# RWKV state of a hybrid mLSTM/RWKV-7 layer: summed in PSUM with an identity product, scaled by ScalarE

## The chip, the core and the metric

The kernel runs on one core of a Trainium2 chip. The metric is the device time of one execution in microseconds (us). Inputs and outputs are fp32 in device memory. The engines are called here as in the profile: PE (TensorE, with PEld for its weight loads), DVE (VectorE), ACT (ScalarE), POOL (GpSimd) and SP (SyncE, which issues nearly all DMAs). Each engine works through its own list of instructions strictly in order, and waits on semaphores for the others.

## The reference, cut to what matters

One layer over 512 latent tokens with a prefix of 256 context tokens, width 2048. One combined input projection feeds two groups of heads: an mLSTM (4 heads) and a RWKV-7 (16 heads of 64, in both directions). Both outputs go through one output projection, then follow a gated ConvFFN (width 5632) and a final RMSNorm. The part that the change touches is the RWKV state, a 64 x 64 matrix for each head and direction:

```
def step(s, xs):
    r_t, w_t, k_t, v_t, kk_t, a_t = xs
    s = (s * w_t[:, :, None, :]
         - einsum("bhvk,bhk->bhv", s, kk_t)[..., None] * (kk_t * a_t)[:, :, None, :]
         + v_t[..., :, None] * k_t[..., None, :])
    return s, einsum("bhvk,bhk->bhv", s, r_t)
...
kk = kk * lax.rsqrt(jnp.sum(kk * kk, axis=-1, keepdims=True) + 1e-12)
k_dir = k_r[:, :, None, :] * (1 + (a - 1) * p["r_k_a"])
y_f, s_f = rwkv7_scan(rh, hd(decay[:, :, 0]), hd(k_dir[:, :, 0]), vh, kk, hd(a[:, :, 0]), state[2], False)
y_b, s_b = rwkv7_scan(rh, hd(decay[:, :, 1]), hd(k_dir[:, :, 1]), vh, kk, hd(a[:, :, 1]), state[3], True)
```

The latent scan starts from the final state of the context's scan. The kernel does it in chunks of 64 tokens.

## The kernel before

**Stages.** The program first computes the modulation vectors and projects the context (to some 400 us of the trace), then interleaves the input projection of the 512 latent tokens with the RWKV work (to some 1400 us), finishes the RWKV and mLSTM heads, runs the output projection in two halves of its input rows (first half from 1650 us, second until 1890 us) and then the ConvFFN.

**Bulk products.** The projections (`proj` at L362, `proj_tm` at L391) split each fp32 operand in a high and a low fp32r part and do three products for each weight block: L370 to L372 with 512 columns, L403 to L405 with 256. `wload` (L337) loads a weight block from memory, ACT casts its high part (`whi`, L299), DVE subtracts to get the low part (`wlo`, L300). Below, these products up to the first of the output projection (L1262) are called bulk products; they wait for nothing of the RWKV work, so they fill PE while that is under way.

**RWKV of a head pair.** Eight pairs of heads, `p` = 0 to 7, two heads on the two halves of the partitions. Each goes through three steps:

1. `prep` (L680): decays, the running products `E1` and `E2` of them, and from them the tiles `KR` (kk and r) and `BK` (minus kk times a, and k). `gC` holds the decay over a whole chunk for each state row. `BK` is scaled by `gC` into `bg` (L756, DVE), transposed on PE (L759, 192 in all) into PSUM, copied by ACT (L763) and written to a buffer in memory (L764). The products of `BK` and `KR` (L747, masked at L750) go to memory too.
2. `tsolve` (L777), for two pairs at once: loads the triangular blocks into the tile `t_X`, inverts them with 30 pairs of DVE operations (L798, L799), then finishes each pair of heads with small PE products (L816, L821), ACT and DVE copies (L818, L823).
3. `chain` (L903): eight `chain_step`s (L841) for a latent pair, four for a context pair, each for one chunk in each direction. A step multiplies the state `u.M` and the values with the chunk's operator, ACT copies the result (`Rs`, L872), a second round of products gives `U` (ACT copy, L880), a third adds up the new state in PSUM, and DVE writes it back: `M = M * gC + sum` (L892). DVE copies out the outputs (L899, L901). There are 96 steps, 88 of them with a new state, four L892 each (352).

The pairs' chains run two at a time for the latent tokens: pairs 0 and 1 while pair 3 is prepared, 2 and 3 with pair 5, 4 and 5 with pair 7, and 6 and 7 after all preparations. The tile `t_X` of the last solve is then taken over by the mLSTM heads 0 and 1 (`mlstm_head`, L540), whose outputs the first half of the output projection needs.

**Another user of DVE.** `ada_late` (L219) computes modulation vectors for later stages: a DMA brings a block of two rows of weights into `am`, one buffer for this stretch, and DVE adds each row into `adacc` (L232, 16 rows of 512 columns for a vector). These stand in DVE's list between the RWKV's instructions.

**Order.** Each engine's list is made by the framework's scheduler, which simulates the program with costs of its own and lets an instruction stand where that simulation has it start. So taking an instruction from one engine to another shifts the lists of all of them.

Of the kernel before, what the change touches and what calls it, by code (L numbers as in the profile page):

```python
# [10 lines left out]
AF = mybir.ActivationFunctionType  # L11
ALU = mybir.AluOpType
# [3 lines left out]
P = 128  # L16
# [80 lines left out]
def body(tc, A, dbg=None):  # L97
    nc = tc.nc
    pe, dve, act, pool, sp = nc.tensor, nc.vector, nc.scalar, nc.gpsimd, nc.sync
# [22 lines left out]
    cst = Pool("cst")  # L122
# [5 lines left out]
    def PS(tag, shape):  # L128
        return ps.tile(list(shape), F32, tag=tag, name=nm(tag), bufs=PB[tag])
# [9 lines left out]
    def cload(name, shape):  # L139
        t = cst("c_" + name, shape)  # L140
        sp.dma_start(t, A[name])
        return t

    rk = Pool("rk")
    rp = Pool("rp")
# [8 lines left out]
    ident = cload("ident", [P, P])  # L154
    bones = cload("bones", [P, P])
    gmask = cload("gmask", [P, 2, P])
    reset = cload("reset", [P, NX + 1])
    bones2 = cload("bones2", [P, 2])
    bconst = cst("bconst", [P, 5])
    for j, v in enumerate((1.0, 1e-6, 1e-12, 64e-5, 0.0)):  # L160
        pool.memset(bconst[:, j:j + 1], v)
# [518 lines left out]
    def prep(p, s, seg, S_d, d=None):  # L680
# [17 lines left out]
        for j, (pt, t, vn) in enumerate(((pw, sg, "w0"), (pa, a, "a0"))):  # L698
            for i, d in enumerate(dirs):
                cs = slice(i * n, i * n + n)  # L700
                pe.matmul(pt[:, cs], s.up[:, j, d, :], (lw, la)[j][seg], start=True, stop=True)
            for i, d in enumerate(dirs):
                cs = slice(i * n, i * n + n)
# [5 lines left out]
        BK = rp("r_BK", [P, 8, 128], 1)  # L709
        E2 = sg  # L710
        gC = rk("r_gC", [P, 8], 16)
# [27 lines left out]
        for hf in range(2):  # L739
# [3 lines left out]
            for c4 in range(4):  # L743
                for h, pg in enumerate(pgs):
                    hs = LOHI[h]
# [6 lines left out]

        for hf in range(2):
            cs = slice(4 * hf, 4 * hf + 4)
            bg = rp("r_cum", [P, 4, 128])
            dve.tensor_tensor(bg, BK[:, cs, :], gC[:, cs, None].to_broadcast([P, 4, 128]), ALU.mult)  # L756
            pb = PS("pre", [P, 4, 128])
            for c4 in range(4):
                pe.transpose(pb[:, c4, :], bg[:, c4, :], ident)  # L759
            bt = rp("r_sg", [P, 4, 128])  # L760
            for h, hs in enumerate(LOHI):
                for js in LOHI:
                    act.copy(bt[hs, :, js], pb[js, :, hs])  # L763
            sp.dma_start(S[:, cs, 3 * kc:3 * kc + 128], bt)  # L764
# [4 lines left out]
        for d in dirs:  # L769
            u = Unit()  # L770
# [70 lines left out]
    def chain_step(us, ops, cs, V, y, first, last):  # L841

        x = us[0].seg == "x"
        kc = us[0].kc
        bank = [PS("R", [P, 8, 64]) for _ in range(2)]
        pos = (0, 1) if cs[0] < cs[1] else (1, 0)
        opened = {}

        def mm(h, half, o, w, rhs):

            hs = LOHI[h]
            out = bank[h][LOHI[half], o, :]
            at = opened.get((h, half))
            f = dict(stop=True, skip_group_check=True)
            if at is None:
                opened[(h, half)] = pe.matmul(out, w[hs], rhs[hs], start=True, **f)
                return
            with tc.issue_after(at.ins):
                pe.matmul(out, w[hs], rhs[hs], start=False, **f)  # L859

        w = [o[:, c % 2] for o, c in zip(ops, cs)]
        kinds = range(2) if x else range(1)
        for src in range(2):
            for k, u in enumerate(us):
                for j in kinds:
                    for h in range(2):
                        o = 2 * kc * src + 64 * j
                        mm(h, h if j == 0 else 1 - h, pos[k], w[k][:, o:o + 64], u.M if src == 0 else V[:, cs[k], :])
        Rs = rk("r_Rs", [P, 2, 64], 3)
        U = rk("r_U", [P, 2, 64], 3)  # L870
        for h, hs in enumerate(LOHI):
            act.copy(Rs[hs], bank[h][hs, 0:2, :])  # L872
        for k, u in enumerate(us):
            for h in range(2):
                mm(h, 1 - h, 2 + pos[k], w[k][:, kc:kc + 64], Rs[:, pos[k], :])
            for h in range(2):
                if not last:
                    mm(h, h, 2 + pos[k], w[k][:, 3 * kc + 64:3 * kc + 128], V[:, cs[k], :])
        for h, hs in enumerate(LOHI):
            act.copy(U[hs], bank[h][LOHI[1 - h], 2:4, :])  # L880
        for k, u in enumerate(us):
            for h in range(2):
                if not last:
                    mm(h, h, 2 + pos[k], w[k][:, 3 * kc:3 * kc + 64], U[:, pos[k], :])
            for h in range(2):
                if x:
                    mm(h, 1 - h, pos[k], w[k][:, kc + 64:kc + 128], U[:, pos[k], :])
        if not last:
            for k, u in enumerate(us):
                g = u.g0 + cs[k]  # L890
                for h, hs in enumerate(LOHI):
                    dve.scalar_tensor_tensor(u.M[hs], u.M[hs], u.gC[hs, g:g + 1], bank[h][hs, 2 + pos[k], :], ALU.mult, ALU.add)  # L892
        if x:
            lo, hi = min(cs), max(cs)
            for h in range(2):
                hs = LOHI[1 - h]
                out = y[hs, lo:hi + 1:hi - lo, :]
                if first:
                    dve.tensor_copy(out, bank[h][hs, 0:2, :])  # L899
                else:  # L900
                    dve.tensor_tensor(out, bank[h][hs, 0:2, :], out, ALU.add)  # L901

    def chain(pairs, mid):  # L903

        x = pairs[0][0].seg == "x"
        nch = pairs[0][0].nch
        Vs, ys = [], []
        for us in pairs:
            Vs.append(chain_v(us[0].p, us[0].seg, nch))
            ys.append(rk("r_yt", [P, 8, 64], 2) if x else None)  # L910
            for u in us:
                if not x:
                    Mst[(u.p, u.d)] = rk("r_M", [P, 64], 16)
                    pool.memset(Mst[(u.p, u.d)], 0.0)
                u.M = Mst[(u.p, u.d)]
        n = nch // 2
        for i in range(n):
            if x and i == 1:
                mid()
            ops = [[chain_load(u, i if u.d == 0 else n - 1 - i) for u in us] for us in pairs]  # L920
            for c in range(2 * i, 2 * i + 2):
                for us, o, V, y in zip(pairs, ops, Vs, ys):
                    chain_step(us, o, (c, nch - 1 - c), V, y, c < nch // 2, x and c == nch - 1)
        if x:
            for us, y in zip(pairs, ys):
                y_d = us[0].y_d = DT("yr_d", [4, P, 128], 8)
                for h in range(2):
                    sp.dma_start(y_d[:, :, 64 * h:64 * h + 64].rearrange("a (b t) v -> t (a b) v", t=64), y[LOHI[1 - h]])
            mid()
# [215 lines left out]
    def ctx_job(p):  # L1145
        do_chain()
        job = []
        for pp in range(p, p + 2):
            s = pair_shared(pp, "c")
            job.append((pp, prep(pp, s, "c", DT("Sc_d", [P, 8, 320], 8)), None))  # L1150
        do_solve()
        solve_q.append(job)

    def x_job(p):
        if p < 2:
            do_chain()
        elif p % 2 == 0:
            do_solve(2)
        else:
            do_chain(2)  # L1160
        s = pair_shared(p, "x")
        S_d = DT("Sx_d", [P, 16, 512], 8)
        us = prep(p, s, "x", S_d, 0) + prep(p, s, "x", S_d, 1)
        job = [(p, us, bonus(p, us[0], us[1], s))]
        if p == 0:
            do_solve()
        solve_q.append(job)
# [185 lines left out]
    last, end = [], iter(())  # L1353
# [147 lines left out]
```

## Time and profile before

| | us |
|---|---|
| median of three runs | 3376.26 |
| fastest and slowest of them | 3374.53, 3378.07 |
| profiled execution | 3379.97 |
| its span, first to last instruction | 3378.2 |
| mean granted TensorE clock | 0.945 of full |

| stretch of the span | what runs there | PE busy of the stretch, clock |
|---|---|---|
| 400 to 883 us | context RWKV, start of the latent projection | 450 of 483 us, 0.94 |
| 883 to 1364.6 us | latent projection with RWKV pairs 1 to 7 | 437 of 482 us, 0.92 and 0.87 |
| 1364.6 to 1650.3 us | last solve, last chain, mLSTM heads 0 and 1 | 170 of 286 us, 0.95 to 0.52 |
| 1650.3 to 3378.2 us | output projection, ConvFFN | 1685 of 1728 us, 0.96 and 0.99 |

PE is busy for 92% of the whole span. A busy share of PE overstates its work, because consecutive products overlap, and a granted clock of 0.5 means that the engine runs at 1.2 GHz where 1.0 is 2.4 GHz.

### The profile page before, as it was taken

The numbers are of one execution on the slowest core, as the hardware profiler recorded it, in microseconds if no ns is written. First come the engines' busy times: TensorE is split into PE (matmuls) and PEld (weight loads), VectorE is DVE, ScalarE is ACT, GpSimd is POOL, SyncE is SP. The second block draws the span as 40 slices with busy tenths as digits, with TensorE's granted clock in tenths as the row PEclk, the third lists the DMA queues.
The fourth block names the chain that finished last, engine by engine and source line by source line (L and its number), as shares of the span: only waits on it lengthen the run. The fifth ranks groups of instructions, "written<-read, shape, count | busy, mean of one in ns | idle before, by whom it ended". The sixth has DMA issues, their size and how long they took to land.

```text
span 3378.2 us, 54574 instructions
## 1 busy us (share of the span) xinstructions
PE 3108.0 (92%) x21030; PEld 2509.7 (74%) x21030; DVE 2165.9 (64%) x4178; ACT 1192.4 (35%) x2414; POOL 59.6 (2%) x113
## 2 busy tenths in 40 slices
PE   8998899999989898657599899999999999999998
PEld 5687777777768687545477688888888888888887
DVE  2587776688688778645644788455555555555657
ACT  4355554344444344222223432222222222322323
POOL 0000100010000000000000000000000000000000
PEclk9999998899989898767799999999999999999999
DMA  8877555557767687565844255222223222222232
GB/s 284 305 243 220 155 159 163 166 174 234 208 208 239 215 247 240 181 197 178 257 153 157 77 199 194 94 94 98 95 95 99 94 96 98 94 98 96 94 100 100
DMA packets 394387, 548.53 MB, mean 162 GB/s; under 512 B 151664, under 2 KB 272776, under 8 KB 393872
## 3 DMA queue, kind: packets, MB, share of 16 engines
q1 hardware_dynamic: 384480, 531.67, 49.3%
q10 hardware_dynamic: 9648, 13.37, 1.1%
q8 instruction: 166, 2.72, 0.3%
q14 instruction: 93, 0.76, 0.1%
HBM read 457.49 MB, written 87.47 MB: 161 GB/s over the span
## 4 chain that ended last, share of the span: by engine, by line
PE 53%; DMA 9%; DVE 6%; ACT 1%; issue 1%; SPq 1%; DVEq 0%; ACTq 0%
PE acc L371 10%; PE acc L372 10%; PE acc L370 10%; PE acc L1376 5%; PE acc L1378 5%; PE acc L1377 5%; DMA am<-in_wmod 3%; PE acc L1262 1%; PE pre L621 1%; PE acc L1263 1%; PE acc L1264 1%; DVE adacc L232 1%; DMA Sx_d<-r_sg 1%; PE R L859 1%; DMA x_d<-ev 1%
## 5 line engine op out<-in xcount | busy, mean ns | idle before, releaser
L299 ACT CAST whi<-wraw 128x512 fp32r<-128x512 f32 (+1 forms) x948 | 569.6, 604 | 1307.7 <-PE acc L371 678.6
L300 DVE TENSOR_TENSOR wlo<-wraw,whi 128x512 fp32r<-128x512 f32 (+1 forms) x948 | 628.4, 666 | 429.0 <-ACT whi L299 423.1
L370 PE MATMUL acc<-H,whi 128*128 128x512 f32 x1920 | 761.2, 396 | 6.1 <-ACT ev L520 4.0
L372 PE MATMUL acc<-H,wlo 128*128 128x512 f32 x1920 | 762.3, 397 | 1.2 <-DVE wlo L300 1.2
L371 PE MATMUL acc<-H,whi 128*128 128x512 f32 x1920 | 760.4, 396 | 0.0
L370 PEld LDWEIGHTS acc<-H,whi 128*128 128x128 f32 x1920 | 363.8, 189 | 87.5 <-ACT ev L520 4.3
L372 PEld LDWEIGHTS acc<-H,wlo 128*128 128x128 f32 x1920 | 364.2, 190 | 82.0 <-issue 4.9
L371 PEld LDWEIGHTS acc<-H,whi 128*128 128x128 f32 x1920 | 364.4, 190 | 78.8 <-issue 2.9
L1380 DVE SCALAR_TENSOR_TENSOR x<-acc,mod,x 128x512 f32<-128x512 f32 (+1 forms) x192 | 135.6, 706 | 221.7 <-PE acc L1378 221.6
L1324 DVE SCALAR_TENSOR_TENSOR f_cv<-upad,fvec,f_cv 128x512 f32<-128x512 f32 x352 | 263.8, 749 | 7.2
L1376 PE MATMUL acc<-fh,whi 128*128 128x512 f32 x640 | 253.2, 396 | 0.0
L1377 PE MATMUL acc<-fl,whi 128*128 128x512 f32 x640 | 253.1, 396 | 0.0
L1378 PE MATMUL acc<-fh,wlo 128*128 128x512 f32 x640 | 253.1, 396 | 0.0
L232 DVE SCALAR_TENSOR_TENSOR adacc<-am,csil,adacc 128x512 f32<-128x512 f32 x240 | 179.4, 748 | 83.7 <-DMA am<-in_wmod 81.6
L403 PE MATMUL acc<-whi,H 128*128 128x256 f32 x512 | 159.8, 313 | 2.2 <-ACT r_E L720 1.5
L405 PE MATMUL acc<-wlo,H 128*128 128x256 f32 x512 | 158.6, 311 | 1.6 <-DVE wlo L300 1.6
L404 PE MATMUL acc<-whi,H 128*128 128x256 f32 x512 | 156.0, 305 | 0.0
L1378 PEld LDWEIGHTS acc<-fh,wlo 128*128 128x128 f32 x640 | 120.2, 188 | 29.1
L1377 PEld LDWEIGHTS acc<-fl,whi 128*128 128x128 f32 x640 | 120.2, 188 | 29.0
L1376 PEld LDWEIGHTS acc<-fh,whi 128*128 128x128 f32 x640 | 120.2, 188 | 29.0
L1262 PE MATMUL acc<-H,whi 128*128 128x512 f32 x256 | 104.6, 414 | 32.4 <-DVE ev L1271 18.6
L750 DVE TENSOR_TENSOR r_Gp<-pre,c_gmask 64x512 f32<-64x512 f32 (+1 forms) x192 | 115.1, 599 | 18.1 <-DMA Sx_d<-r_Gp 11.6
(346 smaller groups left out, 4751.6 us busy)
## 6 DMA issues: line engine op xcount, KB each, us to landing
am<-in_wmod SPq DMA_DIRECT2D x128, 512.0 KB
wraw<-in_wup SPq DMA_DIRECT2D x88, 512.0 KB
wraw<-in_wgate SPq DMA_DIRECT2D x88, 512.0 KB
wraw<-in_wdn SPq DMA_DIRECT2D x88, 512.0 KB
wraw<-in_wcm SPq DMA_DIRECT2D x72, 512.0 KB
r_GK<-Sx_d SPq DMA_DIRECT2D x64, 512.0 KB
wraw<-in_wtm SPq DMA_DIRECT2D x56, 512.0 KB
Sx_d<-r_Gp SPq DMA_DIRECT2D x32, 512.0 KB
```

What stands on the lines that cost most here:

```text
L232: dve.scalar_tensor_tensor(acc, wm[:, k % 2], csil[:, k:k + 1], acc, ALU.mult, ALU.add)
L299: act.copy(hi, t)
L300: dve.tensor_tensor(lo, t, hi.bitcast(F32), ALU.subtract)
L370: pe.matmul(pt[:, :n], hi(k8), H.h(k), start=k == 0, stop=False)
L371: pe.matmul(pt[:, :n], hi(k8), H.l(k), start=False, stop=False)
L372: pe.matmul(pt[:, :n], lo(k8), H.h(k), start=False, stop=k == KT - 1)
L403: pe.matmul(o, H.h(k)[:, xs], hi(k4), start=first, stop=False, skip_group_check=True)
L405: pe.matmul(o, H.h(k)[:, xs], lo(k4), start=False, stop=k == KT - 1, skip_group_check=True)
L1324: dve.scalar_tensor_tensor(cv, u[:, a:a + GH, b:b + GW], fvec[:, f, tap:tap + 1], cv, ALU.mult, ALU.add)
L1376: pe.matmul(pt, hi(m)[:, k, :], th[:, cs], start=k == 0, stop=False)
L1377: pe.matmul(pt, hi(m)[:, k, :], tl[:, cs], start=False, stop=False)
L1378: pe.matmul(pt, lo(m)[:, k, :], th[:, cs], start=False, stop=k == GF - 1)
```

## The change

In `chain_step` the old state is added to the sum in PSUM by a product with an identity matrix (`eye2`), and ACT multiplies the whole sum by `gC` on the way back into `u.M`. DVE no longer takes part in the state. Since the sum is now scaled as a whole, `BK` must reach the chain unscaled, so the scaling into `bg` goes and PE transposes `BK` itself.

```
@@ body
+    eye2 = cst("eye2", [P, 64])
+    for hs in (slice(0, 64), slice(64, 128)):
+        pool.tensor_copy(eye2[hs], ident[hs, hs])
@@ prep
-            bg = rp("r_cum", [P, 4, 128])
-            dve.tensor_tensor(bg, BK[:, cs, :], gC[:, cs, None].to_broadcast([P, 4, 128]), ALU.mult)
             pb = PS("pre", [P, 4, 128])
             for c4 in range(4):
-                pe.transpose(pb[:, c4, :], bg[:, c4, :], ident)
+                pe.transpose(pb[:, c4, :], BK[:, 4 * hf + c4, :], ident)
@@ chain_step, after the products of V with the operator
+            for h in range(2):
+                if not last:
+                    mm(h, h, 2 + pos[k], eye2, u.M)
@@ chain_step, the new state
-                    dve.scalar_tensor_tensor(u.M[hs], u.M[hs], u.gC[hs, g:g + 1], bank[h][hs, 2 + pos[k], :], ALU.mult, ALU.add)
+                    act.activation(u.M[hs], bank[h][hs, 2 + pos[k], :], AF.Copy, scale=u.gC[hs, g:g + 1])
```

In the changed file the lines after these stand one to four lower: the transposition is L760, the new state L896, a solve's product L817.

The counts of instructions differ by this: PE has 352 more products (64 x 64, the identity), DVE has 48 `bg` and 352 state updates fewer, ACT has 352 state writes more and two more loads of its function table, POOL two copies more at the start. The bulk products are the same 4752. The lists differ from the end of the context's projection on. Three places show how.

PE's list around the last transposition of the last prepared pair, before (`pre`, `r_cum`: transposition; `R`: chain; `acc`: bulk products):

```order
L859 MATMUL R_13408<-r_V_12660,r_GK_13279 64x64
L759 MATMUL pre_13661<-c_ident_90,r_cum_13659 128x128 x4
L939 MATMUL pre_13676<-r_rk_2419_13674,r_kd_13518 128x2 x4
L403 MATMUL acc_17052<-whi_17175,H_2684 128x256
L404 MATMUL acc_17052<-whi_17175,H_2685 128x256
L405 MATMUL acc_17052<-wlo_17176,H_2684 128x256
L403 MATMUL acc_17051<-whi_17229,H_2686 128x256
```

And now:

```order
L860 MATMUL R_13485<-r_V_12811,r_GK_13478 64x64
L760 MATMUL pre_13853<-c_ident_90,r_BK_13804 128x128 x4
L760 MATMUL pre_13864<-c_ident_90,r_BK_13804 128x128 x4
L374 MATMUL acc_16854<-H_2690,whi_16895 128x512
L375 MATMUL acc_16854<-H_2689,wlo_16896 128x512
L373 MATMUL acc_16854<-H_2689,whi_16895 128x512
```

The last two transpositions of four now follow each other, and they stand earlier among the bulk products: 147 bulk products stood behind them before (96 of 512 columns, 51 of 256), now it is 389 (197 and 192).

PE's list in front of the first products of the last solve (`R<-t_X,t_Y`), before (L238 and L605 belong to `ada_late` and to mLSTM head 0):

```order
L370 MATMUL acc_17370<-H_2686,whi_17411 128x512
L371 MATMUL acc_17370<-H_2687,whi_17411 128x512
L372 MATMUL acc_17370<-H_2686,wlo_17412 128x512
L238 MATMUL pre_15893<-c_ones_80,adacc_13689 128x1 x4
L605 MATMUL pre_15996<-r_kr_15932,r_KR_15934 128x512
...
L605 MATMUL pre_16012<-r_kr_15932,r_KR_15934 128x512
L816 MATMUL R_13805<-t_X_13801,t_Y_13802 32x32
```

And now:

```order
L407 MATMUL acc_17311<-whi_17488,H_2690 128x256
L408 MATMUL acc_17311<-wlo_17489,H_2689 128x256
L406 MATMUL acc_17310<-whi_17488,H_2689 128x256
L817 MATMUL R_14008<-t_X_14004,t_Y_14005 32x32
L817 MATMUL R_14009<-t_X_14004,t_Y_14005 32x32
```

Before, no bulk product was left behind this place. Now 131 are (96 of 512 columns, 35 of 256), 99 of them (64 and 35) ahead of the solve's second pair of heads. Between the last transposition and this place stand 101 bulk products of 512 and 157 of 256 columns.

ACT's list at the first step of the last chain, before (`t_X<-R`: solve; `t_X<-t_X`: mLSTM head 0):

```order
L818 COPY t_X_13801<-R_13879 32x512
L818 COPY t_X_13801<-R_13880 32x512
L872 COPY r_Rs_13984<-R_13966 64x128
L872 COPY r_Rs_13984<-R_13967 64x128
L880 COPY r_U_13985<-R_13966 64x128
L880 COPY r_U_13985<-R_13967 64x128
L589 ACTIVATE t_X_15941<-t_X_15941 128x128
L594 ACTIVATE t_X_15941<-t_X_15941,tokb_132 128x256
```

And now:

```order
L873 COPY r_Rs_14187<-R_14170 64x128
L302 CAST whi_17940<-wraw_17938 128x512
L884 COPY r_U_14188<-R_14169 64x128
L884 COPY r_U_14188<-R_14170 64x128
L592 ACTIVATE t_X_16200<-t_X_16200 128x128
L597 ACTIVATE t_X_16200<-t_X_16200,tokb_135 128x256
L592 ACTIVATE t_X_16200<-t_X_16200 128x128
L302 CAST whi_17944<-wraw_17938 128x512
L896 ACTIVATE r_M_7521<-R_14169,r_gC_12607 64x64
L896 ACTIVATE r_M_7523<-R_14169,r_gC_12691 64x64
L896 ACTIVATE r_M_7521<-R_14170,r_gC_12607 64x64
L896 ACTIVATE r_M_7523<-R_14170,r_gC_12691 64x64
```

Weight casts now stand among the step's copies, and the state writes behind them. In DVE's list, the additions of `ada_late` keep their places beside the RWKV work: 98 stood ahead of the last solve before and 96 now, 126 and 122 ahead of its end, 170 and 170 ahead of the output projection's first result (L1271).

## Rows read from the trace of the kernel before

**Rows 1.** The page's engine line: busy us, share of the span, instructions.
```profile
PE 3108.0 (92%) x21030; PEld 2509.7 (74%) x21030; DVE 2165.9 (64%) x4178; ACT 1192.4 (35%) x2414; POOL 59.6 (2%) x113
```

**Rows 2.** Stretches: us; busy PE, PEld, DVE, ACT, POOL (instructions); clock; DMA share; GB/s.
```profile
883.00:1244.70 361.70, 327.69 (x3977) 266.19 (x3970) 286.44 (x637) 155.95 (x354) 6.80 (x20) 0.92 0.72 223
...
1244.70:1364.60 119.90, 109.57 (x1500) 89.01 (x1498) 87.86 (x200) 51.84 (x127) 2.15 (x5) 0.87 0.73 239
...
1402.10:1472.10 70.00, 22.67 (x334) 15.01 (x336) 40.90 (x90) 6.58 (x14) 0.00 (x0) 0.52 0.52 152
...
1472.10:1650.30 178.20, 112.86 (x1190) 83.38 (x1186) 93.48 (x247) 57.09 (x178) 1.72 (x8) 0.72 0.67 212
```

**Rows 3.** Waits of PE, 400 to 1400 us: total us, times, longest.
```profile
PE pre L759 <- DVE r_cum L756: 10.6, 4, 6.3
...
PE R L859 <- ACT r_U L880: 10.4, 9, 1.7
...
PE R L856 <- DVE r_M L892: 1.7, 5, 0.7
```

**Rows 4.** DVE groups, 400 to 1650 us: xcount, busy, mean ns, idle before.
```profile
L892 DVE SCALAR_TENSOR_TENSOR r_M<-r_M,r_gC,R 64x64 f32<-64x64 f32 x352 | 87.5, 278 | 28.5 <-PE R L859 21.9 <-ACT r_U L880 2.7
...
L756 DVE TENSOR_TENSOR r_cum<-r_BK,r_gC 128x512 f32<-128x512 f32 x41 | 28.1, 685 | 2.8 <-PE pre L759 2.3
```

**Rows 5.** ACT groups, 400 to 1650 us, the same columns.
```profile
L299 ACT CAST whi<-wraw 128x512 fp32r<-128x512 f32 x195 | 120.0, 618 | 187.6 <-PE acc L371 114.7 <-PE acc L404 51.4 <-DVE t_X L799 8.1
...
L763 ACT COPY r_sg<-pre 64x256 f32<-64x256 f32 x168 | 61.7, 367 | 70.8 <-PE pre L759 29.8 <-DMA Sx_d<-r_sg 25.7 <-PE acc L404 6.5
...
L880 ACT COPY r_U<-R 64x128 f32<-64x128 f32 x192 | 49.8, 260 | 80.7 <-PE R L859 75.1 <-DVE t_X L799 1.6 <-ACT ev L520 0.4
...
L872 ACT COPY r_Rs<-R 64x128 f32<-64x128 f32 x192 | 49.8, 259 | 98.6 <-PE R L859 88.5 <-DVE t_T L798 3.6 <-DVE ev L173 3.1
...
L520 ACT COPY ev<-acc 128x256 f32<-128x256 f32 x32 | 11.2, 373 | 9.2 <-DMA v_x<-ev 3.2 <-DMA vx_d<-ev 2.6 <-PE acc L405 1.6
...
L626 ACT ACTIVATE r_KR<-pre,m_dn 128x256 f32<-128x256 f32 x8 | 3.8, 472 | 8.3 <-DVE m_dn L625 8.3
```

**Rows 6.** A stretch of bulk products alone, columns as in Rows 2.
```profile
2000.00:2500.00 500.00, 500.00 (x2198) 410.20 (x2197) 304.35 (x458) 137.03 (x224) 0.00 (x0) 1.00 0.35 118
```

**Rows 7.** Timeline of PE: start us, us, engine, line, tiles, form, xcount.
```profile
1366.68 0.45 PE L859 MATMUL R<-r_Rs,r_GK 64*64 64x64 f32 x8
...
1367.06 0.38 PE L404 MATMUL acc<-whi,H 128*128 128x256 f32 x1
...
1371.99 0.28 PE L405 MATMUL acc<-wlo,H 128*128 128x256 f32 x1
...
1372.36 0.28 PE L405 MATMUL acc<-wlo,H 128*128 128x256 f32 x1
...
1471.61 0.97 PE L859 MATMUL R<-r_U,r_GK 64*64 64x64 f32 x16 [0.36 <-ACT r_U L880]
```

**Rows 8.** Timeline of PE: last transposition, last solve, start of the output projection.
```profile
1364.02 0.66 PE L759 MATMUL pre<-c_ident,r_cum 128*128 128x128 f32 x4
...
1424.95 1.84 PE L238 MATMUL pre<-c_ones,adacc 128*128 128x1 f32 x8 [22.87 <-DVE adacc L232]
...
1447.87 1.92 PE L816 MATMUL R<-t_X,t_Y 32*32 32x32 f32 x64 [9.65 <-DVE t_X L810]
...
1464.78 1.92 PE L816 MATMUL R<-t_X,t_Y 32*32 32x32 f32 x64 [11.22 <-DVE t_X L810]
...
1650.34 0.80 PE L1262 MATMUL acc<-H,whi 128*128 128x512 f32 x1 [18.55 <-DVE ev L1271]
```

**Rows 9.** Timeline of DVE: start and end of the last solve.
```profile
1372.41 0.09 DVE L794 MEMSET t_X<- 128x32 f32 x1 [1.20 <-DMA t_X<-Sx_d]
...
1470.62 1.40 DVE L823 COPY t_Y<-R 32x512 f32<-32x512 f32 x2
```

**Rows 10.** Tile adacc on DVE, 1364 to 1651 us: idle before it, times.
```profile
  DMA am<-in_wmod: 46.3, 25
```

## The prediction

> **What bounds the kernel now.** I read the engine line first: PE is busy for 92% of the span, so the time lies with PE and only its idle stretches can be shortened [rows 1]. The stretches come next. While pairs are prepared, PE is busy for 327.7 of 361.7 us and 109.6 of 119.9 us, at a clock of 0.92 and 0.87; DVE for 286.4 and 87.9, ACT for 156.0 and 51.8. From 1402.1 us the picture turns: 22.7 of 70.0 us, then 112.9 of 178.2 us, at a clock of 0.52 and 0.72, thus nearer to 1.2 than to 2.4 GHz [rows 2]. There the bulk products are used up, and PE waits: 22.87 us ahead of L238, 9.65 and 11.22 ahead of the last solve's products [rows 8]. From the end of the last solve on DVE, 1472.0 us [rows 9], it takes 178 us to the output projection at 1650.3 [rows 8]. So the end of the latent part is set by a string: last preparation (last transposition 1364.0), solve (first product 1447.9, 83.9 us later), end of the solve, mLSTM heads 0 and 1 with the last chain beside them, output projection. The bulk products lie beside it and are all done some 46 us before the solve reaches PE. What follows 1650 us is not touched by the change.
>
> While pairs are prepared PE hardly waits for what the change removes: 10.6 us for the scaled BK, 1.7 us for the new state, each over 1000 us [rows 3]. So the removed DVE work gains little directly; what counts is where it lets the lists put the RWKV work.
>
> **Part by part.**
>
> *DVE loses* 352 state updates of 278 ns, 97.9 us, and 48 scalings of 685 ns, 32.9 us [rows 4]: 131 us on an engine that is busy for three quarters of the stretch [rows 2]. Off PE's path by themselves, but the preparation and the solve run through DVE.
>
> *PE gains* 352 identity products of 64 x 64. Rows of the same form: eight take 0.38 us up to the next product, 48 ns each; sixteen took 0.97 us at the low clock, 61 ns [rows 7]. The lower end is nothing, where they fall into a wait of PE for the Rs copy beside them. I take 48, the nearest row at the full clock. In PE's list 288 of them stand ahead of the last transposition: 13.8 us, from 0 to 17.6.
>
> *ACT gains* 352 writes of 64 x 64 from PSUM with a scale read per partition. No row shows that size. A copy of 128 columns takes 259 ns and one of 256 takes 367, so 64 columns come to about 205 ns; a scale per partition adds 99 ns (472 against 373 for 256 columns) [rows 5]. So 304 ns each, 107 us; the ends are 259 (no pointer cost) and 472 ns, 91 to 166 us. ACT is busy for 43% of the stretch [rows 2] and has room for it; the casts of weights wait behind, which is a rival below.
>
> The row says thus that ACT needs 26 ns more than DVE for the same piece. The Trainium skill (ScalarE: Activation LUTs, Rules for kernel authors) speaks against the move: multiplications belong on VectorE. Its figures (same page, What ACT_TABLE_LOAD costs: 186 ns plus 0.833 ns per element, and 93 ns for a pointer operand) would make 332 ns, 117 us in all; by it the rival of the late casts weighs a little more, and the sum stays.
>
> *The order.* This is the main term. PE's list has 242 fewer bulk products ahead of the last transposition (101 of 512 columns, 141 of 256). A product of 512 columns takes 500 / 2198 = 0.2275 us [rows 6], one of 256 takes 0.37 / 3 = 0.123 us [rows 7]: 23.0 + 17.3 = 40.3 us of PE time that now lie behind the place. PE is nearly full up to there, so the last preparation comes earlier by this, less 13.8 us for the identity products, plus some 5 us of the waits for the scaled BK (half of 10.6, since PE still waits for BK itself): 31.5 us, at about 1332.5.
>
> *The solve.* On PE the way from there to the first solve product is now 101 x 0.2275 + 157 x 0.123 = 42 us of bulk and some 5 us of chain products (104 x 48 ns). The solve took 83.9 us through DVE and memory [rows 8], nearly all of it after DVE's first operation at 1372.4 [rows 9]; DVE's list holds about the same beside it. So DVE decides still, PE waits for some 35 us, and the product comes at 1332.5 + 83.9 = 1416.4 us, 31.5 earlier. Then 99 bulk products stand ahead of the solve's second half: 64 x 0.2275 + 35 x 0.123 = 18.9 us, where 16.9 us lay between the two halves before [rows 8]; with about 4 us of the solve's own products the second half is late by 6 us. That is the price of the bulk that fills the hole.
>
> *The tail.* Behind the solve DVE does 56 state updates less (7 steps, 2 pairs, 4 each), 15.6 us, while 4 more additions of `ada_late` stand there (48 for 44) with two more DMAs to wait for. In the tail DVE waits 46.3 us for these DMAs [rows 10]; the 44 additions, 22 blocks of two rows, went in 178.2 us, 8.1 us a block. Two more cost from 3 us (their work) to 16 us. I take 11, and a net gain of 5 us.
>
> *Nothing*: the two copies on POOL at the start lie beside the first weight loads. The two more table loads on ACT are covered by its idle time; uncovered they would cost under 3 us.
>
> **The sum.** 40.3 - 13.8 + 5 - 6 + 5 = 30.5 us. The profiled execution took 3380.0 us, which makes 3349.5; the median of the runs lies 3.7 us lower, so the forecast is 3346 us.
>
> **The rivals.**
>
> *A. Larger gain.* The solve itself shortens too, because DVE is relieved of the state updates of the chain that runs beside it and PE arrives before it. Were the 83.9 us to come down to the 47 us that PE needs, the second half's lateness aside, 37 us more would go: from 3310 to 3330 us. For it: DVE was the engine that PE waited for there. Against it: most of DVE's load in the solve (additions, finalisation, splits) stays.
>
> *B. Given back, no change.* The start of the tail comes earlier, and the tail grows: both `ada_late` blocks at 8.1 us (16 instead of 11), no gain from fewer updates, bulk at the low clock between the two halves of the solve (18.9 twice, 19 more), identity products at 61 ns. Then 40.3 - 17.6 - 16 - 6 + 5 = 6 us are left without the clock term, and less than nothing with it: 3370 to 3383 us. For it: the clock was 0.52 in that place and the stream of DMAs ran through the whole tail. Against it: PE is fuller there now.
>
> *C. Slower.* The state write stands in ACT's list among casts and copies, and casts stand behind state writes. ACT waits already 88.5 us for the first and 75.1 us for the second round of products, 164 us over 192 waits for 96 steps, 0.85 us each [rows 5]. A third wait in each step delays the casts by that, and a cast ahead of the write (0.618 us) delays the state. If PE has to sit out 0.75 us in each of the 74 state updates ahead of the last solve's chain, that is 56 us against the gain of 30.5: 3402 us. It decides from 0.41 us a step on. For it: PE already waits 10.4 us for U [rows 3], and the steps stand closer together now. Against it: ACT is idle for more than half of the stretch [rows 2], and three buffers of cast weights stand between a cast and its product.
>
> **How the numbers follow.** A gain from 7 to 55 us as forecast: 0.53. Case A, beyond: 0.13. Case B, within the 0.2% (6.8 us) that a measurement here can tell from no change: 0.15. Case C: 0.19. So faster 0.66, same 0.15, slower 0.19. The forecast's own range is 3321 to 3369 us. The range for 8 in 10 goes from 3300, where half of case A is in, to 3393, where half of case C is: it leaves out 0.06 and 0.10.
>
> **What would show it.** In the changed profile the last transposition (L760) should be at about 1332 us and the first product of the last solve at about 1416, with a wait of PE for DVE's transposition (L811) of some 30 us ahead of it; the second at about 1439, and bulk products between the two. The state writes (L896) should take about 300 ns, 352 times, and PE's waits for ACT's U and Rs copies should grow by under 15 us. PE should be busier between 1402 and 1472 us, at a higher clock. The output projection should start near 1620 us, and from there on the spans should be equal. The forecast is wrong if the last transposition is not earlier (the lists then ran ahead of what DVE and ACT can do), if waits of PE for `whi` or `wlo` appear (case C), or if the stretch from the end of the solve to the output projection is longer than 190 us (case B).

## The result, and the profile after

The changed kernel takes 3407.79 us (median of its runs, 3406.0 to 3409.31), 1.0093 times the kernel before (95% interval 1.007 to 1.0116): 31.5 us slower, where 30.5 us faster was forecast. The profiled execution has a span of 3407.5 us, 29.3 more than before, at the same mean clock of 0.945.

The engine line of the page after, against [rows 1]:

```profile
PE 3135.3 (92%) x21734; PEld 2542.4 (75%) x21734; DVE 2061.3 (60%) x3778; ACT 1288.6 (38%) x2768; POOL 50.2 (1%) x115
```

DVE lost 104.6 us and ACT gained 96.2. The forecast had 131 and 107: it multiplied counts by mean durations, while neighbouring instructions overlap (the 352 state updates were busy for 87.5 us [rows 4], not 97.9). PE gained 27.3 us, nearly the whole loss. PE has 704 records more for 352 identity products: a product of this form is two records.

The stretches after, cut near the places of [rows 2] (883 us; a transposition; the last transposition; some 38 us behind it; the end of the solve; columns as there):

```profile
883.00:1252.00 369.00, 322.86 (x3858) 262.94 (x3857) 242.40 (x492) 169.63 (x440) 4.50 (x18) 0.85 0.67 202
1252.00:1372.40 120.40, 101.73 (x1443) 83.30 (x1442) 71.60 (x133) 62.27 (x167) 0.98 (x4) 0.91 0.74 236
...
1410.60:1487.10 76.50, 69.51 (x673) 58.98 (x673) 55.00 (x114) 25.55 (x46) 0.00 (x0) 0.96 0.78 229
1487.10:1675.00 187.90, 117.69 (x1321) 90.25 (x1319) 86.56 (x199) 73.66 (x238) 1.75 (x8) 0.73 0.66 209
```

The hole ahead of the solve is filled as forecast: PE is busy for 69.5 of 76.5 us there at a clock of 0.96, where it was 22.7 of 70.0 at 0.52. But the two stretches ahead of it, which should have become shorter by what was taken out of them, became longer, with PE less busy (322.9 of 369.0 us against 327.7 of 361.7) and at a clock of 0.85 against 0.92. DVE, which was to be relieved, is relieved: 242 us against 286. PE got nothing of it.

These rows can be split. Work is called here PE's busy time times the granted clock, and low clock the rest of the busy time. From 883 us to the last transposition PE did 367 us of work against 397 before, as the list said; but it was idle for 64.8 us against 44.3, and the low clock took 58 us against 40. So 30 us of work went, and 38 us of idle time and low clock came.

PE's timeline after, the places of [rows 8]:

```profile
1371.81 0.63 PE L760 MATMUL pre<-c_ident,r_BK 128*128 128x128 f32 x4 [0.80 <-DVE r_Gp L753]
...
1456.34 1.20 PE L817 MATMUL R<-t_X,t_Y 32*32 32x32 f32 x64
...
1675.00 0.80 PE L1266 MATMUL acc<-H,whi 128*128 128x512 f32 x1 [18.09 <-DVE ev L1275]
```

The last transposition is 7.8 us late (forecast: 31.5 early), the solve 8.5, the output projection 24.7; from there to the end it is 1732.5 us against 1727.9. (The place taken for the output projection is where its products go on behind the wait for `ev`; single ones stand ahead of it, in the kernel before from 1542.8 us.) The long waits ahead of the solve's products are gone.

PE's waits after, 400 to 1400 us, against [rows 3] (total us, times, longest):

```profile
PE pre L241 <- ACT r_sg L764: 12.1, 3, 9.0
PE pre L750 <- DVE r_Gp L753: 11.7, 8, 4.0
PE R L860 <- ACT r_U L884: 11.7, 6, 3.3
PE R L857 <- DVE r_yt L905: 10.8, 9, 2.7
PE pre L760 <- DVE r_Gp L753: 9.0, 7, 3.5
PE pre L704 <- ACT r_sg L764: 8.7, 5, 4.2
PE R L857 <- DVE r_yt L903: 7.1, 5, 3.0
...
PE R L857 <- ACT r_M L896: 4.6, 3, 2.4
PE acc L408 <- DVE wlo L303: 4.3, 4, 2.0
```

The same waits before, as far as [rows 3] does not show them:

```profile
PE pre L747 <- DVE r_Gp L750: 7.4, 11, 1.6
PE pre L701 <- ACT r_sg L763: 6.9, 3, 3.3
...
PE R L856 <- DVE r_yt L899: 4.2, 8, 0.9
...
PE pre L238 <- ACT r_sg L763: 3.4, 2, 2.2
...
PE pre L759 <- DVE r_Gp L750: 2.7, 4, 1.1
...
PE R L856 <- DVE r_yt L901: 1.5, 4, 0.7
```

All lines of this view add up to 112.6 us against 78.4. The wait for the scaled BK (10.6 us) has gone, and the waits for `r_Gp` have grown by as much (20.7 us against 10.1). The waits for ACT's `r_sg` grew from 10.3 to 24.0 us, those for DVE's y copies from 5.7 to 17.9. For the y copies, DVE's own waits say why (all of 400 to 1660 us):

```profile
DVE r_yt L903 <- ACT r_M L896: 22.5, 12, 10.2
...
DVE r_yt L905 <- ACT r_M L896: 12.2, 13, 3.6
```

The y copy and the state write read the same bank. On one engine they stood one behind the other; now DVE waits for ACT, 34.7 us, and the bank comes free later. Before, DVE had no such wait. How this looks at one place, first on ACT, then on DVE:

```profile
934.66 0.72 ACT L668 ACTIVATE r_kk<-r_kr,c_vecs 128x512 f32<-128x512 f32 x1 [4.37 <-DMA r_kr<-kr_x]
935.41 0.55 ACT L884 COPY r_U<-R 64x128 f32<-64x128 f32 x2
935.98 0.63 ACT L670 ACTIVATE r_t<-r_kk 128x512 f32<-128x512 f32 x1
936.52 0.53 ACT L873 COPY r_Rs<-R 64x128 f32<-64x128 f32 x2
937.07 1.05 ACT L896 ACTIVATE r_M<-R,r_gC 64x64 f32<-64x64 f32 x4
```

```profile
937.61 0.29 DVE L903 COPY r_yt<-R 64x128 f32<-64x128 f32 x1 [2.44 <-ACT r_M L896]
```

One ACT instruction of a preparation waits 4.37 us for a transfer, and the U copy, the Rs copy, the state write and DVE's y copy all stand behind it.

The state write costs what was estimated (columns as [rows 5]):

```profile
L896 ACT ACTIVATE r_M<-R,r_gC 64x64 f32<-64x64 f32 x352 | 94.3, 304 | 58.0 <-PE R L860 54.6
```

304 ns is the value worked out from rows. The Trainium skill's figures (ScalarE: Activation LUTs, What ACT_TABLE_LOAD costs) make 332 ns, an estimate; the measurement decides for 304.

Who waits for the identity products, from the view of their tile:

```profile
who waited for it (us, times):
  ACT r_U L884: 54.5, 40
```

The U copy reads the other half of the same bank, no result of an identity product, and waits for it all the same: the program puts it behind every product that stands ahead of it in the code for this bank. In the built program each of the 176 U copies of steps with a state write waits for the last identity product of its bank. So in the lists the products stand inside the step. That this makes the step longer does not follow: the view names the product that came last, and ACT's idle time ahead of all U copies is no longer than before, 75.2 us against 80.7 [rows 5]:

```profile
L884 ACT COPY r_U<-R 64x128 f32<-64x128 f32 x192 | 49.9, 260 | 75.2 <-PE R L860 71.4 <-ACT ev L523 0.4
```

### The profile page after: what moved, and what is told of

Same layout as the page of the kernel before. It is cut to its first block, busy times and chain, and to the rows that moved or that the text cites. A ratio compares the mean times of both kernels' runs of the same rounds, so it can differ in the third digit from the quotient of the medians.

```text
span 3407.5 us, 55869 instructions
## 1 busy us (share of the span) xinstructions
PE 3135.3 (92%) x21734; PEld 2542.4 (75%) x21734; DVE 2061.3 (60%) x3778; ACT 1288.6 (38%) x2768; POOL 50.2 (1%) x115
## 4 chain that ended last, share of the span: by engine, by line
PE 68%; DMA 16%; DVE 8%; ACT 4%; issue 2%; SPq 1%; ACTq 0%; DVEq 0%; POOL 0%; POOLq 0%
PE acc L374 11%; PE acc L375 11%; PE acc L373 11%; DMA am<-in_wmod 5%; PE acc L1380 5%; PE acc L1382 4%; PE acc L1381 4%; PE R L860 2%; PE pre L750 2%; PE pre L198 2%; DVE adacc L235 1%; PE acc L1266 1%; PE acc L1267 1%; PE acc L1268 1%; DMA Sx_d<-r_Gp 1%
## 5 line engine op out<-in xcount | busy, mean ns | idle before, releaser
L408 PE MATMUL acc<-wlo,H 128*128 128x256 f32 x512 | 157.9, 311 | 8.4 <-DVE wlo L303 7.9
```

The source lines that it names most:

```text
L408: pe.matmul(o, H.h(k)[:, xs], lo(k4), start=False, stop=k == KT - 1, skip_group_check=True)
```

## The experiments

Theories at the start. 1: ACT's state write is the cost. 2: the identity products are PE time. 3: each edit sorts all lists anew, and the waits that come of it outweigh the edit; later 4, with the products' work of some 17 us and a scatter of the lists of some 0.4% beside it. 5 came after the first eight runs: the products' place ahead of the U copies counts. Ratios are against runs of the kernel before beside them, with 95% intervals.

**Parts alone.** e1, the scaling back on DVE:

```diff
-act.activation(u.M[hs], bank[h][hs, 2 + pos[k], :], AF.Copy, scale=u.gC[hs, g:g + 1])
+dve.tensor_scalar(u.M[hs], bank[h][hs, 2 + pos[k], :], u.gC[hs, g:g + 1], None, ALU.mult)
```

> The changed kernel, but the state is scaled out of PSUM by DVE (352 tensor_scalar) instead of ACT; identity products and unscaled BK stay. Theory 1 (ACT's write is the cost: the state stands in ACT's list behind casts, and DVE's y copies and the bank behind it): the loss goes away, 3360 to 3382 us, DVE's waits on r_yt <- r_M (34.7 us) gone, PE's waits for r_yt back from 27 to under 12 us. Theory 2 (the identity products are PE time, 48 ns each and more where a group of them is cut off from others): 3393 to 3408 us, no more than 15 us better than the changed kernel. Theory 3 (every edit sorts all lists anew, the preparation is set by strings through DVE and ACT, and the bulk products only fill): anything from 3370 to 3410, the last transposition again at 1365 to 1375 us.

1.0126 (1.0107 to 1.0145). No better than with ACT, though DVE's y copies no longer wait for the state write: against theory 1, in one list.

e2, the changed kernel without the products, so that the old state is left out of the sum:

```diff
-                    mm(h, h, 2 + pos[k], eye2, u.M)
```

> The changed kernel without the 352 identity products (the old state is thus left out of the sum). Theory 1 (ACT's write is the cost): 3395 to 3406 us, the products hardly count. Theory 2 (PE time of the products): 3375 to 3391 us, 17 to 33 us less than the changed kernel, PE's busy time down by 17 to 30 us. Theory 3: a change of any sign, up to 20 us.

0.9956 (0.994 to 0.9971), and e3, the kernel before with as many added:

```diff
+                    mm(h, h, 2 + pos[k], zero2, u.M)
```

> The kernel before with 352 products of the same form added at the same place (a tile of zeros times the state, so that nothing is added to the sum); everything else as before, the state on DVE. Theory 1: the products fall into PE's wait beside them, less than 8 us more, 3376 to 3384 us. Theory 2: 17 to 33 us more, 3393 to 3409 us. My prediction's price of 48 ns each would make 3390 to 3393.

1.0159 (1.0139 to 1.0179). Both say 46 to 54 us, beyond even theory 2. The engine lines of e2 and e3:

```profile
PE 3090.8 (93%) x21030; PEld 2501.8 (75%) x21030; DVE 2060.0 (62%) x3778; ACT 1287.4 (39%) x2768; POOL 52.4 (2%) x115
```

```profile
PE 3142.0 (92%) x21734; PEld 2546.8 (75%) x21734; DVE 2173.3 (64%) x4178; ACT 1197.2 (35%) x2416; POOL 54.3 (2%) x114
```

e4, the y copies moved ahead of the state write in the code:

```diff
-        if not last: (state writes)
         if x: (y copies)
+        if not last: (state writes)
```

> The changed kernel, with the y copies of a step written ahead of its state writes in the code, so that DVE's y copy no longer waits for ACT's state write of the same bank (and the state write waits for the y copy instead). Theory 1 in the form that the y copies hold the banks: 3388 to 3398 us, DVE's wait r_yt <- r_M (34.7 us) gone and PE's wait for r_yt down from 27 to 12 us, ACT's wait for r_M longer. Theory 2: within 6 us of the changed kernel, 3402 to 3414 us.

1.0052 (1.0034 to 1.0069), 14 us better than the changed kernel. It fits theory 1's weaker form, but it is one list.

**The same work, sorted anew.** e5 to the kernel before, e6 to the changed one:

```diff
-            for k, u in enumerate(us):
-                for h, hs in enumerate(LOHI):
+            for h, hs in enumerate(LOHI):
+                for k, u in enumerate(us):
```

> The kernel before with the two loops around the state update changed places (half outside, direction inside): the same 352 instructions, another order of four neighbours in the code, but the scheduler's lists are sorted anew (some 7,000 rows of PE's list stand elsewhere). Theory 3 (each edit sorts the lists anew, and the waits that come of it are worth more than the edit): a change of either sign, 10 to 40 us. Rival (the lists are as good as each other, only the work counts): within 8 us of the kernel before, ratio 0.9975 to 1.0025.

> The changed kernel with the same exchange of the two loops around the state write: no work more or less, the lists sorted anew. Theory 3: 10 to 40 us away from the changed kernel's ratio of 1.0093, to either side, thus under 1.006 or over 1.012. Rival: ratio 1.006 to 1.012.

e5 1.0042 (1.0028 to 1.0056), as theory 3 had it; e6 1.0082 (1.0068 to 1.0097), as its rival had it. e15 and e16 do it with another exchange, of the halves of the Rs products:

```diff
-            for h in range(2):
+            for h in (1, 0):
                 mm(h, 1 - h, 2 + pos[k], w[k][:, kc:kc + 64], Rs[:, pos[k], :])
```

> The kernel before with the same exchange of the halves of the Rs products: a second new sorting of its lists. By theory 4 0.996 to 1.008, as the first (1.0042); were it within 0.002 of 1, the first exchange would not have been a fair measure of the scatter.

> The changed kernel with the same exchange, a second new sorting. Theory 4: 1.000 to 1.012, around 1.006. Theory 5: over 1.006 again, since every U copy waits for identity products in any sorting (the two so far are 1.0093 and 1.0082).

e15 1.0022 (1.0009 to 1.0035), e16 1.0086 (1.0065 to 1.0107). So the kernel before has the best of its three lists, which makes up 0.2% of the loss; the three lists of the changed kernel lie close together. From mean to mean (1.0021 to 1.0087) the change costs 0.66%, 22 us.

**No identity product, BK unscaled.** e7 and e8 scale the old state early on ACT or POOL:

```diff
+act.activation(ms, u.M, AF.Copy, scale=u.gC[:, g:g + 1])   # e8: pool.tensor_scalar
-dve.scalar_tensor_tensor(u.M[hs], u.M[hs], u.gC[hs, g:g + 1], bank[h][hs, 2 + pos[k], :], ALU.mult, ALU.add)
+dve.scalar_tensor_tensor(u.M[hs], bank[h][hs, 2 + pos[k], :], u.gC[hs, g:g + 1], Ms[k][hs], ALU.mult, ALU.add)
```

> A version that leaves BK unscaled without an identity product: ACT scales the old state into a tile of its own early in the step (176 instructions of 128 x 64, from memory to memory), and DVE adds it to the scaled product as before (352). DVE loses the 48 scalings (32.9 us), PE does the work of before. If the identity products are what costs (theory 2, 46 to 54 us so far), this should be faster than before: 0.985 to 0.998. Theory 3: anything from 0.985 to 1.012, whatever the work.

> The same with the early scaling on POOL, which is busy for 2% of the span, so that ACT's list holds nothing new. By theory 2 0.985 to 0.998, as good as the version with ACT or better by up to 10 us; if POOL takes over 0.6 us for a piece, the state waits for it and the gain is lost: 0.998 to 1.005. Theory 3: anything from 0.985 to 1.012.

1.0076 (1.0058 to 1.0095) and 1.0048 (1.003 to 1.0067). e7 misses theory 2's range. e8 lies in the range for slow pieces on POOL, but the reason given there is not seen: half of the pieces took under 0.45 us (the mean, 697 ns, comes from longer ones, up to 8.6 us), and the only waits of DVE's state write (400 to 1660 us) are for PE, 18.9 us:

```profile
L872 POOL TENSOR_SCALAR r_Ms<-r_M,r_gC x176: 437/446/8595, 274.5 to 1577.6; 128x64 f32<-128x64 f32 x176
```

```profile
DVE r_M L897 <- PE R L857: 18.9, 9, 6.5
```

Taking the 32.9 us of scaling off DVE brought nothing in either list.

e9 and e10 are e2 and e3 with the loops exchanged, e11 puts 384 products on zeros into the preparation instead:

```diff
+pe.matmul(pb[hs, c4, 0:64], zero2[hs], bg[hs, c4, 0:64], start=True, stop=True, skip_group_check=True)
```

> The changed kernel without identity products (old state left out of the sum) and with the two loops of the state write exchanged, which only sorts the lists anew. Theory 4 (the products cost their work, 17 us by busy time times granted clock, and the rest is a scatter of the lists of some 0.4%): 0.994 to 1.004, the 0.9956 of the first list without them was partly luck. Theory 5 (they also lengthen the string of each step, because all 176 U copies wait for the last identity product of their bank; 40 to 50 us in all): again 0.993 to 0.998, under 0.997 most likely.

> The kernel before with the 352 added products on zeros, and the two loops of the state update exchanged. Theory 4: 1.003 to 1.011 (work 0.5%, lists 0.4%). Theory 5: again 1.012 to 1.018.

> The kernel before with 384 products of 64 x 64 on zeros elsewhere: eight ahead of the four transpositions of each half of BK, in the bank that these overwrite, 48 groups. They are no part of a step of the chain. Theory 5: only their work, 384 x 48 ns = 18 us, and thus clearly less than 352 of them in the chain: 1.003 to 1.007. Theory 4: 1.001 to 1.010, the same as in the chain within the scatter of the lists.

1.0039 (1.0022 to 1.0055), 1.0049 (1.0035 to 1.0064) and 1.0128 (1.0111 to 1.0145). e9 and e10 lie in theory 4's ranges and miss theory 5's. The 46 and 54 us of e2 and e3 were thus half a matter of the list: two lists of the same work lie up to 1.1% apart. e11 missed both ranges: products that are no part of a step cost as much as those in it. They stand in another string there, between BK and the transpositions; whether that is why is not shown.

**The place of the products.** e12 moves them behind the U copies; e13 and e14 sort e12 anew by the two exchanges:

```diff
-                    mm(h, h, 2 + pos[k], eye2, u.M)      # ahead of the U copies
         for h, hs in enumerate(LOHI):
             act.copy(U[hs], bank[h][LOHI[1 - h], 2:4, :])
+        for k, u in enumerate(us):
+                    mm(h, h, 2 + pos[k], eye2, u.M)
```

> The changed kernel with the identity products written behind the U copies instead of ahead of them: none of the 176 U copies waits for one any more, they stand with the U products. Theory 5: part of the loss comes back, 1.000 to 1.005. Theory 4: 1.004 to 1.014, as the changed kernel within the scatter of the lists.

> The version with the identity products behind the U copies, with the loops of the state write exchanged: no work more or less, the lists sorted anew. Theory 4 (scatter of the lists, its 0.9949 was a lucky list): 1.000 to 1.012. Theory 5 (the place of the products is what counted, because no U copy waits for them): 0.992 to 0.999.

> The same version with the two halves of the Rs products issued in the other order (half 1 ahead of half 0), a second new sorting. Theory 4: 1.000 to 1.012. Theory 5: 0.992 to 0.999.

0.9949 (0.9932 to 0.9966), 1.0014 (1.0 to 1.0028), 1.0032 (1.0019 to 1.0044). e12 lies below both ranges; e13 and e14 lie in theory 4's and miss theory 5's. Still all three lie below all three of the changed kernel, by 0.9% or 30 us in the mean. In e12 the products' tile view reads:

```profile
its engine sat idle before it (us, times) until:
  ACT r_U L881: 29.5, 23
...
who waited for it (us, times):
  POOL r_rk L941: 0.9, 1
```

Now the products wait for the U copy, and no copy for them. e12 is the fastest version measured that keeps the whole state, and beats both kernels; its two twins beat only the changed one. So its lead on the kernel before is a lucky list, as the mean of the three, 0.9998, says.

e17 moves the products of V and BK of the kernel before behind the U copies, e18 those and the identity products of the changed one:

```diff
-                    mm(h, h, 2 + pos[k], w[k][:, 3 * kc + 64:3 * kc + 128], V[:, cs[k], :])
         (U copies)
+                    mm(h, h, 2 + pos[k], w[k][:, 3 * kc + 64:3 * kc + 128], V[:, cs[k], :])
```

> The kernel before, with the products of V and scaled BK (352, into the same half of the bank as the state) written behind the U copies instead of ahead of them, so that a U copy waits for the Rs products alone. No product more or less. Theory 5 (what stands ahead of the U copies in a step costs its time): faster than before, 0.990 to 0.998. Theory 4: 0.996 to 1.008.

> The changed kernel with both the products of V and BK and the identity products behind the U copies. Theory 5: as good as or better than the version with the identity products alone behind (0.9949): 0.988 to 0.996. Theory 4: 0.996 to 1.012.

0.999 (0.9979 to 1.0) and 1.0129 (1.011 to 1.0148). Both miss theory 5's ranges, and e18 theory 4's as well. e17 lies within the scatter, and e18 is against theory 5: no copy waits for an identity product there either (the same 0.9 us), and it is among the slowest. So the wait of the U copies isn't the rule. In e18's profile the loss is not in waits: PE is idle for 252 us of the span, less than in any list of the tables below but e2 (250), and it has 3018 us of work and 147 of low clock, more than any of them. Why was not tried further.

Where the time lies, from the profiled executions (us; means over the lists; "last transposition" is the start of its last product on PE, "solve" from there to DVE's last copy of the solve, "tail" from there to the output projection):

| version, lists | last transposition (lowest to highest) | solve | tail | rest | span |
|---|---|---|---|---|---|
| before, 3 | 1370 (1364 to 1373) | 103 | 179 | 1730 | 3382 |
| changed, 3 | 1368 (1366 to 1372) | 118 | 186 | 1733 | 3405 |
| products behind U, 3 | 1340 (1329 to 1352) | 104 | 195 | 1732 | 3370 |
| no products, 2 | 1334 (1321 to 1348) | 122 | 176 | 1732 | 3363 |

And PE's span split in three, summed over windows of 10 us: work (busy time times granted clock), what the lower clock took, and idle time:

| version, lists | work | low clock | idle | span |
|---|---|---|---|---|
| before, 3 | 2984 | 125 | 273 | 3382 |
| changed, 3 | 3006 | 132 | 267 | 3405 |
| products behind U, 3 | 2994 | 116 | 260 | 3370 |
| no products, 2 | 2987 | 115 | 261 | 3363 |

The changed kernel has 21 us more work on PE and the same loss beside it (399 us against 398). Without the products the loss falls by 22 us in these profiles. But each row is one execution of each list, and they were not all typical: e2's was the fastest of its 12 (9.6 us below the median), e5's the slowest of its 8 (8.5 above). By the ratios the versions without products and with the products behind the U copies lie both 8 us below the mean of the kernel before (0.9998 against 1.0021), within the scatter of the lists, and some 11 us of loss are saved instead of 22. That is what the relief of DVE and the new order are worth in the mean; with the products ahead of the U copies this gain is gone.

## Why the prediction was wrong

**The order (40.3 us), with the price of the identity products (13.8 us): here it failed.** The list did hold the bulk products where it was said, but the last transposition came at 1371.8 us instead of 1332.5. The step that failed is this one: PE is nearly full up to there, so the last preparation comes earlier by the work that was taken out. It holds PE's idle time and its clock at what they were. The runs show both moving instead. Split over windows of 10 us as above, from the start to the last transposition (means over the lists, us):

| version, lists | work | low clock | idle | last transposition |
|---|---|---|---|---|
| before, 3 | 1174 | 74 | 122 | 1370 |
| changed, 3 | 1137 | 89 | 142 | 1368 |
| products behind U, 3 | 1118 | 79 | 143 | 1340 |
| no products, 2 | 1125 | 71 | 138 | 1334 |

The work fell by 37 us, and 35 us of idle time and low clock took its place; the three changed lists lie close together (1366 to 1372). The waits shown above account for a part of the idle time: DVE's y copies behind ACT's state write, and ACT's `r_sg`. Why the clock was lower is not known.

Most of the term is there when the identity products do not stand ahead of the U copies: 1320.6 us in e2 without them (1348 in its twin), 1329.2 in e12 behind the copies (1339 and 1352 in its twins). Against the lists without products they cost some 34 us at this place (1368 against 1334), between 18 and 52 by the single lists, where I put 13.8 and at most 17.6. How they cost it stays open. That the U copies wait for them is not it: PE is idle as long with the products behind the copies (143 us against 142), and what is saved is work and low clock. From the end of an Rs copy to the start of a U copy it is 3.8 to 4.1 us in the mean in the three lists of the kernel before, 3.6 to 4.3 in the changed ones, 3.9 to 4.0 with the products behind. Nor does the place decide everywhere: e18 comes to 1383, e17 to 1340, and with the same products added to the kernel before e3 comes to 1389 and e10 to 1348.

Two faults of size are in the price of the products as PE time. I took records for products: eight records are four products, so that the row of the prediction says 95 ns each, 27 us for the 288. And a product's price depends on its group. PE's timeline after, at one place:

```profile
577.74 0.28 PE L406 MATMUL acc<-whi,H 128*128 128x256 f32 x1
577.95 0.45 PE L860 MATMUL R<-r_U,r_GK 64*64 64x64 f32 x8
578.33 0.39 PE L407 MATMUL acc<-whi,H 128*128 128x256 f32 x1
```

Four products (eight records) hold PE for 0.38 us here, 95 ns each. In the mean over all 352 the work rose by 21 us, 60 ns each: my 48 was near by chance. And the bulk ahead of the last transposition, as a count, is a poor clock: in the built lists it makes 737, 730 and 732 us of products for the kernel before and 697, 674 and 668 for the changed one, for nearly the same moment.

**The scaled BK (5 us).** The wait went, and `r_Gp` took its place (9.0 us ahead of the same transpositions): nothing gained (2.7 before; the other wait for it grew by 4.3).

**ACT's write.** 304 ns as estimated, and taking it back to DVE brought nothing in the one list tried (e1). That DVE's y copies would wait for it was not foreseen: 34.7 us on DVE, for which e4 gives back 14 us in one list.

**The solve.** It started DVE's way 9.5 us late (1381.9) and took 74.4 us to its first product, 75.5 before: DVE decides, as said. The second half came 24.3 us behind the first instead of 16.9, 7.4 late; I had 6.

**The tail (a gain of 5).** 187.9 us instead of 178.3. Without the products it is 174 to 177 in both lists, so the relief of DVE is worth about what was said; the tails of the three changed lists are 6 to 14 longer than that. That the identity products of the last chain are the reason is not shown: behind the U copies, the tail is longer still (195).

**The rivals.** C named nearly the time (3402), by luck in the main. Its waits are seen in part: between 400 and 1400 us PE's waits grew by 34 us where C had 56, and 12 of the 34 are for the y copies behind ACT's write. But with the state on DVE the kernel is no faster (e1), and PE waited only 1.6 us for `whi` and 4.3 for `wlo` (L408) up to 1400 us. B had its part as far as, in the mean, the solve is 15 us and the tail 7 us longer; that this is the work that no longer stood ahead of them is not shown. A did not occur. No rival of mine let the clock fall ahead of the last transposition.

What stays open: why the clock fell and PE idled more ahead of the last transposition, why the products' place ahead of the U copies costs what it does in these lists, why e18 is slow, and how much of any one list's time is the edit's. Single lists of one work lie up to 1.1% apart here (e3 and e10), the interval of a measurement is 0.2%.

## What to carry to other kernels

Where a scheduler sorts the lists, an edit's effect is the mean over several equal sortings: exchange two loops, twice, on both sides, before one explains half a per cent. Try an added product at another place of the step before giving up on it: here the place was worth 30 us in the mean of three lists, for a reason that stays open. Price a small product by the group that it stands in, and count products, not records. Work that is moved out from ahead of a milestone shortens the way only as far as idle time and clock stay as they were: split PE's time into work, low clock and idle time before and after, and forecast all three.

## Not expected of the hardware

Between bulk products of 128 x 128 at the full clock, the group of eight records of 64 x 64 above held PE for 0.38 us, and this one of sixteen for 0.39: up to this size, how many products such a group has hardly counts. Groups of 32 records took 0.62 us and more.

```profile
1079.29 0.39 PE L373 MATMUL acc<-H,whi 128*128 128x512 f32 x1
1079.61 0.46 PE L860 MATMUL R<-r_U,r_GK 64*64 64x64 f32 x16
1080.00 0.50 PE L374 MATMUL acc<-H,whi 128*128 128x512 f32 x1
```
